# Copies inside a branch that is never taken, issued by GpSimd instead of ScalarE

## The chip, the cores and the metric

The kernel runs on one core of one Trainium2 chip. The metric is the device time of one execution in microseconds; of three runs the median is 1869.39 us (1868.79 to 1871.61). The profile is of one further execution, traced by the hardware profiler.

## The reference, cut to what matters

Two blocks follow each other on 256 tokens of width 1024. The first has two layers, each a token mixer (attention, then a pooling mixer) and a mixture of experts; the second block (recurrent mixers and dense feed-forward layers) is not touched. The change lies in the mixture of experts, which both layers have, each with weights of its own:

```python
scores = sigmoid(hf @ router_w)              # 256 tokens x 32 experts
e_idx  = top_k(where(best_group, scores + router_bias, -inf), 2)
gate   = scores[e_idx] / sum(scores[e_idx])
# every expert e, on the tokens that chose it:
y[e]   = (silu(x[e] @ w1[e]) * (x[e] @ w3[e])) @ w2[e]     # 1024 -> 512 -> 1024
out    = sum over the two chosen experts of gate * y[e]
```

Weights are drawn at random, so how many tokens choose one expert is not bounded by the shapes: the worst case is 256.

## The kernel before, in words

The 32 experts of a layer are worked off in 16 pairs (`for p in range(NPAIR)` in `experts`). Each expert gets 64 slots for tokens (`cap`), so that a pair fills the 128 partitions. For a pair TensorE runs

- `up` (L1190): the gathered tokens `hg` against w1 and w3, four chunks of weights of 2 MB, 16 matmuls for each chunk;
- `turned` (L1203): four transposes of the activated product `u`, which VectorE copies into the tile `uT` (L1205);
- `down` (L1217): `uT` against w2, two chunks of 2 MB, 16 matmuls for each; its two halves are written into the tiles `yh` (by ScalarE, L1228 in layer 0 and L1224 in layer 1) and `yl` (by VectorE, L1229 and L1226);
- `spread_out` (L1242 and L1237): adds the result to the tokens; it is done one pair later.

Every second pair the tokens of the next two pairs are gathered (L1155, with `oh` made by VectorE at L1141 and L1144). TensorE's order is that of the code; the other engines' instructions are ordered by a scheduler.

**The stream of weights.** All chunks of the kernel stand in one list. `prefetch` (L206) issues the next one from SyncE (SP) as soon as one of the rings `ringa`, `ringb`, `ringc` has a free slot (ten slots in layer 0, seven in most of layer 1). Each of these DMAs raises one of eight semaphores, DMAHW0 to DMAHW7, taken in turn, and waits for the DMA that used the same semaphore eight places earlier; so at most eight are in flight.

**The overflow branch.** Where an expert gets more than 64 tokens, the rest is computed in `overflow`, called once in each layer, in pair 9 after `up` and before `turned`. It loads the largest count into a register on every engine (L1287) and branches (L1288). The body uses the tiles `hg`, `oh`, `uT`, `yh` and `yl` as its own, so that the instructions behind the branch which write these tiles wait for the body's copies. Those copies (L1299, L1313, L1318, L1325) use DMA semaphores like any other DMA. On the way that leaves the body out, the semaphores that the body would have raised are raised by hand, so that both ways end at the same counts: each by one instruction that first waits until the semaphore stands at the count at which the body would have found it. With the counts of this input neither layer takes the branch: no instruction of its body shows in the trace.

Of the kernel before, what the change touches and what calls it, by code (L numbers as in the profile page):

```python
# [19 lines left out]
T = 256  # L20
# [144 lines left out]
class Net:  # L165
# [1112 lines left out]
    def overflow(self, l, htok, gate, slot, mint, cap, yacc, wp, pp):  # L1278


        nc, tc, A = self.nc, self.tc, self.A
        h = wp.tile([128, KT, T], F32, name="hg")
        idr = wp.tile([128, 2, 4, 64], F32R, name="oh").rearrange("p a b n -> p (a b n)")[:, 0:128]
        ug = wp.tile([128, 4, 128], F32, name="uT").rearrange("p a n -> p (a n)")
        u, gr = ug[:, 0:T], ug[:, T:2 * T]
        w, wd = (wp.tile([128, D], F32, name=n) for n in ("yh", "yl"))
        rv = nc.values_load(mint[0:1, 0:1], min_val=0, max_val=T)  # L1287
        with tc.If(rv > cap):  # L1288
            with ExitStack() as es:
                dp = es.enter_context(tc.tile_pool(name=f"ovd{l}", bufs=1, space=DRAM))  # L1290
                rows = dp.tile([NE, T], F32, name="rows")
                nc.scalar.copy(idr, self.ident)
                ov, rsb = w[:, 0:2 * NE].rearrange("p (a e) -> p a e", a=2), wd[0:NE, 0:T]
                nc.vector.scalar_tensor_tensor(ov, slot, float(cap), gate, op0=OP.is_gt, op1=OP.mult)
                pr = pp.tile([NE, T], F32, name="e1", bufs=2)
                for tt in range(2):
                    nc.tensor.transpose(pr[:, tt * 128:(tt + 1) * 128], ov[:, tt, :], self.ident)
                nc.vector.tensor_copy(rsb, pr)
                nc.scalar.dma_start(rows, rsb)  # L1299
                for k in range(KT):  # L1300
                    ph = pp.tile([128, T], F32, name="e1", bufs=2)
                    for tt in range(2):
                        for i in range(2):
                            nc.tensor.matmul(ph[:, tt * 128:(tt + 1) * 128], htok[i][:, tt, k * 128:(k + 1) * 128], idr,
                                             start=i == 0, stop=i == 1)
                    nc.vector.tensor_scalar(h[:, k, :], ph, self.mscale[l][:, 1, k:k + 1], self.shift(l, 1)[:, k:k + 1],
                                            op0=OP.mult, op1=OP.add)
                wk = w.rearrange("p (k n) -> p k n", k=KT)
                we = A["exp"][l].rearrange("q c p (a b n) -> q c p a b n", a=4, b=2)
                with tc.For_i(0, NPAIR, 1) as pv:  # L1310
                    for ab in range(2):
                        src = rows[:, :].rearrange("(q a) t -> q a t", a=2)[ds(pv, 1), ab, :]
                        nc.scalar.dma_start(gr, src.to_broadcast([128, T]))  # L1313
                        for ft in range(4):
                            ps = []
                            for i in range(2):
                                for c in range(2):
                                    nc.scalar.dma_start(  # L1318
                                        wk[:, 4 * c:4 * c + 4, :],
                                        we[ds(pv, 1), 2 * i + c, :, :, ab, ft * 128:(ft + 1) * 128]  # L1320
                                        .rearrange("q p a n -> (q p) a n"))
                                ps.append(pp.tile([128, T], F32, name="e0", bufs=2))
                                self.dense(ps[i], wk, 0, h)
                            for hf in range(2):
                                nc.scalar.dma_start(wd[:, 512 * hf:512 * hf + 512],  # L1325
                                                  we[ds(pv, 1), 4 + hf, :, ft, ab, :].rearrange("q p n -> (q p) n"))
                            nc.scalar.activation(u, ps[0], AF.Silu)
                            nc.vector.tensor_tensor(u, u, ps[1], op=OP.mult)
                            nc.vector.tensor_tensor(u, u, gr, op=OP.mult)
                            if l:  # L1330
                                nc.vector.tensor_tensor(wd, wd, self.gb, op=OP.mult)
                                for tt in range(2):
                                    for hf in range(2):
                                        nc.tensor.matmul(yacc[tt][hf], u[:, tt * 128:(tt + 1) * 128], wd[:, 512 * hf:512 * hf + 512],
                                                         start=False, stop=False, skip_group_check=True)
                            else:
                                for nt in range(KT):
                                    nc.tensor.matmul(yacc[:, nt, :], wd[:, nt * 128:(nt + 1) * 128], u,
                                                     start=False, stop=False, skip_group_check=True)
# [1078 lines left out]
```

## Time and profile before

| | |
|---|---|
| time, median of three runs | 1869.39 us |
| the profiled execution | 1871.96 us |
| its span, first to last instruction | 1870.2 us |
| TensorE's granted clock, mean | 0.967 of full speed |
| TensorE busy | 1738.4 us, 93% of the span |
| VectorE, ScalarE, GpSimd busy | 791.0, 532.7, 163.6 us |
| read from HBM | 579.65 MB, 311 GB/s over the span |

TensorE passes the branch at 476 us of the span in layer 0 and at 975 us in layer 1. A row of a timeline or a wait names the engine, the line of the kernel and the tile that is written; `SPq` is SyncE's own instruction queue. A value in brackets is the idle time of the engine just before, and what ended it.

### The profile page before, as it was taken

How to read it: one execution, taken by the hardware profiler on the slowest of the kernel's cores; microseconds unless marked ns; L12 is line 12 of the kernel's file. 1: busy time of each engine (PE TensorE's matmuls, PEld its weight loads, DVE VectorE, ACT ScalarE, POOL GpSimd, SP SyncE). 2: the span in 40 equal slices, each digit the busy share in tenths (PEclk: the TensorE clock that was granted, in tenths of full speed). 3: DMA queues.
4: the chain of work that ended last, by engine and by line, in shares of the span. 5: the costliest groups of instructions: out<-in, count | busy, mean ns of one | idle time of the engine just before them, and what ended most of it. 6: DMA issues, size and time to landing. Idle time of an engine off the chain costs nothing. (4 is left out here: it accounts for less than half of the span.)

```text
span 1870.2 us, 26586 instructions
## 1 busy us (share of the span) xinstructions
PE 1738.4 (93%) x11262; PEld 1165.4 (62%) x11262; DVE 791.0 (42%) x1552; ACT 532.7 (28%) x950; POOL 163.6 (9%) x249
## 2 busy tenths in 40 slices
PE   6998999999589989999995999999999999999998
PEld 4666544443234445444433434779999989989997
DVE  4687422211112125222522242665655566565554
ACT  2321211111001122111200101445644466564443
POOL 0000000000000000000440340223000002200000
PEclk9999999999789999999997999989999999999999
DMA  9998899999999996999996999615344533344531
GB/s 397 426 422 317 366 427 427 426 428 426 426 390 426 426 428 273 421 426 410 427 426 273 421 413 426 256 68 193 150 177 180 196 143 136 136 158 181 214 127 66
DMA packets 41665, 582.52 MB, mean 311 GB/s; under 512 B 4625, under 2 KB 4753, under 8 KB 5953
## 3 DMA queue, kind: packets, MB, share of 16 engines
q1 hardware_dynamic: 41328, 580.46, 75.1%
q8 instruction: 92, 1.51, 0.3%
q10 hardware_dynamic: 208, 0.26, 0.1%
q14 instruction: 37, 0.30, 0.0%
HBM read 579.65 MB, written 1.05 MB: 311 GB/s over the span
## 5 line engine op out<-in xcount | busy, mean ns | idle before, releaser
L243 DVE TENSOR_TENSOR wlo<-ringa,whi 128x1024 fp32r<-128x1024 f32 x192 | 228.5, 1231 | 174.6 <-ACT whi L242 174.6
L1190 PE MATMUL e<-ringb,hg 128*64 128x512 f32 x1056 | 233.9, 594 | 1.2 <-DMA ringb<-in_exp 1.2
L242 ACT CAST whi<-ringa 128x1024 fp32r<-128x1024 f32 x192 | 191.4, 1050 | 144.2 <-issue 54.9
L266 PE MATMUL ph<-hlo,whi 128*128 128x256 f32 x704 | 198.8, 282 | 1.2 <-DVE hlo L557 1.2
L265 PE MATMUL ph<-hhi,whi 128*128 128x256 f32 x704 | 198.6, 282 | 0.0
L267 PE MATMUL ph<-hhi,wlo 128*128 128x256 f32 x704 | 198.4, 282 | 0.0
L1197 DVE TENSOR_TENSOR u<-u,e 128x512 f32<-128x512 f32 x32 | 22.0, 688 | 384.1 <-PE e L1190 384.1
L1190 PEld LDWEIGHTS e<-ringb,hg 128*64 128x64 f32 x1056 | 79.6, 137 | 146.2 <-issue 141.8
L1190 PE MATMUL e<-ringa,hg 128*64 128x512 f32 x592 | 134.2, 599 | 17.7 <-DVE yl L1229 16.0
L266 PEld LDWEIGHTS ph<-hlo,whi 128*128 128x128 f32 x704 | 133.9, 190 | 2.4 <-DVE hlo L557 1.6
L265 PEld LDWEIGHTS ph<-hhi,whi 128*128 128x128 f32 x704 | 133.9, 190 | 0.8
L267 PEld LDWEIGHTS ph<-hhi,wlo 128*128 128x128 f32 x704 | 133.9, 190 | 0.0
L1467 POOL TENSOR_TENSOR ringa<-ringa 128x128 f32<-128x128 f32 (+1 forms) x86 | 45.8, 545 | 813.5 <-DVE ringa L1463 703.3
L1217 PE MATMUL e<-ringa,uT 128*64 128x512 f32 x384 | 91.4, 623 | 19.4 <-DVE uT L1205 15.8
L1190 PEld LDWEIGHTS e<-ringa,hg 128*64 128x64 f32 x592 | 45.1, 138 | 100.9 <-issue 81.7
L1217 PE MATMUL e<-ringb,uT 128*64 128x512 f32 x416 | 95.8, 606 | 8.8 <-DVE uT L1205 7.2
L1190 PE MATMUL e<-ringc,hg 128*64 128x512 f32 x400 | 88.4, 592 | 1.8 <-DMA ringc<-in_exp 1.8
L1228 ACT ACTIVATE yh<-e,gs 128x512 fp32r<-128x512 f32 x32 | 21.9, 687 | 226.0 <-PE e L1217 195.3
L1160 ACT ACTIVATE hg<-e,mod,msc 128x256 f32<-128x256 f32 x64 | 36.2, 565 | 164.9 <-DVE hg L1162 157.1
L1224 ACT CAST yh<-u 128x512 fp32r<-128x512 f32 x32 | 19.8, 618 | 217.6 <-DVE u L1223 217.6
L1155 PE MATMUL e<-oh,hth 128*128 128x256 f32 x256 | 68.9, 305 | 12.1 <-DVE oh L1141 7.5
L1229 DVE SCALAR_TENSOR_TENSOR yl<-e,gs,yh 128x512 fp32r<-128x512 f32 x32 | 23.9, 750 | 123.7 <-ACT yh L1228 123.7
(588 smaller groups left out, 3209.5 us busy)
## 6 DMA issues: line engine op xcount, KB each, us to landing
ringb<-in_exp SPq DMA_DIRECT2D x92, 2048.0 KB, 20.0
ringa<-in_exp SPq DMA_DIRECT2D x61, 2048.0 KB, 19.7
ringc<-in_exp SPq DMA_DIRECT2D x39, 2048.0 KB, 24.0
ringa<-in_f SPq DMA_DIRECT2D x32, 2048.0 KB, 7.5
ringb<-in_ada SPq DMA_DIRECT2D x15, 2048.0 KB, 16.2
ringa<-in_ada SPq DMA_DIRECT2D x9, 2048.0 KB, 21.9
ringa<-in_cin SPq DMA_DIRECT2D x8, 2048.0 KB, 7.4
ringa<-in_attn SPq DMA_DIRECT2D x3, 2048.0 KB, 28.2
```

What stands on the lines that cost most here:

```text
L242: nc.scalar.copy(hi[:, o], raw[:, o])
L243: (eng or nc.vector).tensor_tensor(lo[:, o], raw[:, o], hi[:, o], op=OP.subtract)
L265: mm(ps, wh, ah, start=start, stop=False, **kw)
L266: mm(ps, wh, al, start=False, stop=False, **kw)
L267: mm(ps, wl, ah, start=False, stop=stop, **kw)
L1155: nc.tensor.matmul(pd[:, i, :], htok[h][:, tt, k * 128:(k + 1) * 128], oh[:, tt, :], start=tt + h == 0, stop=tt + h == 2)
L1160: nc.scalar.activation(hg[q][:, k, :], pd[:, i, :], AF.Identity, scale=sc[:, k:k + 1], bias=sh[:, k:k + 1])
L1190: nc.tensor.matmul(ps[s, :], h[:, kt, o:o + 64], w[:, k, ab, :], start=kt == 0, stop=kt == KT - 1)
L1197: nc.vector.tensor_tensor(u, u, ph[1], op=OP.mult)
L1217: nc.tensor.matmul(py[s, :], uT[:, ft, s], w[:, ft, ab, :], start=ft == 0, stop=ft == 3)
L1229: nc.vector.scalar_tensor_tensor(lo, py, g, hi, op0=OP.mult, op1=OP.subtract)
L1467: nc.gpsimd.tensor_tensor(o, a, b, op=op)
```

## The change

The four kinds of copies in the branch's body are issued by GpSimd (POOL) instead of ScalarE. DMAs that GpSimd issues use another set of eight semaphores, DMASW0 to DMASW7.

```diff
                 nc.vector.tensor_copy(rsb, pr)
-                nc.scalar.dma_start(rows, rsb)
+                nc.gpsimd.dma_start(rows, rsb)
...
                     for ab in range(2):
                         src = rows[:, :].rearrange("(q a) t -> q a t", a=2)[ds(pv, 1), ab, :]
-                        nc.scalar.dma_start(gr, src.to_broadcast([128, T]))
+                        nc.gpsimd.dma_start(gr, src.to_broadcast([128, T]))
...
-                                    nc.scalar.dma_start(
+                                    nc.gpsimd.dma_start(
                                         wk[:, 4 * c:4 * c + 4, :],
...
-                                nc.scalar.dma_start(wd[:, 512 * hf:512 * hf + 512],
+                                nc.gpsimd.dma_start(wd[:, 512 * hf:512 * hf + 512],
```

SyncE's queue in layer 0, from the end of the branch on, before (the first row is the way around the body; `ringb_3084` is the next weight chunk):

```order
L1288 UNCONDITIONAL_BRANCH [waits DMAHW0_49,DMAHW1_49,DMAHW2_49,DMAHW3_49,DMAHW4_49,DMAHW5_49,DMAHW6_49,DMAHW7_49]
L206 DMA ringb_3084<-in_exp 128x4096 [waits DMAHW3_49,PE_49]
L206 DMA ringb_3097<-in_exp 128x4096 [waits DMAHW4_49,PE_49]
L206 DMA ringa_3110<-in_exp 128x4096 [waits DMAHW5_49,DMAHW0_49,PE_49]
L206 DMA ringa_3120<-in_exp 128x4096 [waits DMAHW6_49,DMAHW1_49,PE_49]
```

The same place after the change:

```order
L1288 UNCONDITIONAL_BRANCH
L206 DMA ringb_3084<-in_exp 128x4096 [waits DMAHW0_49,PE_49]
L206 DMA ringb_3097<-in_exp 128x4096 [waits DMAHW1_49,PE_49]
L206 DMA ringa_3110<-in_exp 128x4096 [waits DMAHW2_49,PE_49]
L206 DMA ringa_3120<-in_exp 128x4096 [waits DMAHW3_49,PE_49]
```

The eight waits at the end of the branch are gone; the DMAs keep their order.

VectorE's queue behind the branch in layer 0, before (`uT_3071` and `yl_3074` belong to pair 9):

```order
L1144 TENSOR_TENSOR oh_3169<-oh_3169,gate_1350 128x256 [waits DVE_49]
L1205 COPY uT_3071<-e1_3066 128x512 [waits DMAHW2_49,PE_49]
L1144 TENSOR_TENSOR oh_3169<-oh_3169,gate_1350 128x256 [waits DVE_49]
L1229 SCALAR_TENSOR_TENSOR yl_3074<-e0_3075,gs_2299,yh_3073 128x512 [waits DMAHW1_49,DMAHW2_49,DMAHW0_49,Activation_49]
L1229 SCALAR_TENSOR_TENSOR yl_3074<-e0_3088,gs_2299,yh_3073 128x512 [waits Activation_49]
```

And after:

```order
L1144 TENSOR_TENSOR oh_3169<-oh_3169,gate_1350 128x256 [waits DVE_49]
L1205 COPY uT_3071<-e1_3066 128x512 [waits DMASW2_49,PE_49]
L1144 TENSOR_TENSOR oh_3169<-oh_3169,gate_1350 128x256 [waits DVE_49]
L1229 SCALAR_TENSOR_TENSOR yl_3074<-e0_3075,gs_2299,yh_3073 128x512 [waits DMASW1_49,DMASW2_49,DMASW0_49,Activation_49]
L1229 SCALAR_TENSOR_TENSOR yl_3074<-e0_3088,gs_2299,yh_3073 128x512 [waits Activation_49]
```

The order is the same; the waits on the body's copies now ask for the other set of semaphores. ScalarE's copy into `yh` changes in the same way.

GpSimd's queue at the end of the branch in layer 1, before (what follows is its work for the second block):

```order
L1288 UNCONDITIONAL_BRANCH
L1467 TENSOR_TENSOR ringa_4749<-ringa_4749 128x4x32 [waits PE_49] x2
L1467 TENSOR_TENSOR ringa_4749<-ringa_4749 128x4x32 [waits Pool_49]
L1467 TENSOR_TENSOR ringa_4749<-ringa_4749 128x4x32 [waits PE_49] x2
L1467 TENSOR_TENSOR ringa_4749<-ringa_4749 128x128 [waits Pool_49]
```

And after:

```order
L1288 ISA [waits DMASW4_49,DMASW5_49,DMASW3_49,DMASW6_49,DMASW2_49,DMASW7_49,DMASW1_49,DMASW0_49]
L1288 UNCONDITIONAL_BRANCH
L1467 TENSOR_TENSOR ringa_4749<-ringa_4749 128x4x32 [waits PE_49] x2
L1467 TENSOR_TENSOR ringa_4749<-ringa_4749 128x4x32 [waits Pool_49]
L1467 TENSOR_TENSOR ringa_4749<-ringa_4749 128x4x32 [waits PE_49] x2
```

One instruction has come in, at the end of the way around the body (in layer 0 too): it raises the eight DMASW semaphores (`INC_SWDGE_SEM` in the trace). In layer 0 the counts that it waits for are zero, in layer 1 those that its own instance in layer 0 has left; no other DMA of the kernel uses this set. The body on GpSimd has grown by about a hundred rows in each layer, that on ScalarE has shrunk by as many.

## Rows read from the trace of the kernel before

**Rows 1.** The page's second part: busy tenths of the DMA engines in 40 slices

```profile
DMA  9998899999999996999996999615344533344531
```

**Rows 2.** All instructions of L1288: count, duration in ns (min/median/max), first and last start

```profile
L1288 SPq EVENT_SEMAPHORE  x16: 17/17/17, 486.6 to 1003.8; - x16
L1288 POOLq COMPARE_BRANCH  x2: 45/45/45, 208.4 to 956.7; - x2
...
L1288 PEldq COMPARE_BRANCH  x2: 6019/6028/6037, 476.0 to 975.2; - x2
```

**Rows 3.** SyncE's waits, 470 to 540 and 975 to 1035: total us, times, longest

```profile
SPq L1288 <- SPq L1288: 38.7, 8, 5.0
...
SPq L1288 <- SPq L1288: 25.2, 1, 25.2
```

**Rows 4.** SyncE's timeline in layer 0: start, us to the group's end, instruction

```profile
432.63 10.13 SPq L206 DMA_DIRECT2D ringb<-in_exp  x3
...
481.74 40.09 SPq L206 DMA_DIRECT2D ringb<-in_exp  x3
...
635.82 0.33 SPq L206 DMA_DIRECT2D ringc<-in_exp  x1
```

**Rows 5.** DMAs issued at 481.74 and at 635.82: last column us to landing

```profile
ringb<-in_exp SPq DMA_DIRECT2D x1, 2048.0 KB, 39.1
...
ringc<-in_exp SPq DMA_DIRECT2D x1, 2048.0 KB, 26.3
```

**Rows 6.** TensorE's timeline around the branch of layer 0

```profile
466.98 3.65 PE L1190 MATMUL e<-ringa,hg 128*64 128x512 f32 x16 [1.33 <-DMA ringa<-in_exp]
...
497.29 9.30 PE L1217 MATMUL e<-ringb,uT 128*64 128x512 f32 x32 [7.19 <-DVE uT L1205]
522.54 8.62 PE L1190 MATMUL e<-ringa,hg 128*64 128x512 f32 x32 [15.95 <-DVE yl L1229]
```

**Rows 7.** VectorE's timeline there

```profile
490.34 0.42 DVE L1144 TENSOR_TENSOR oh<-oh,gate 128x256 f32<-128x256 f32 x1
496.54 0.69 DVE L1205 COPY uT<-e 128x512 f32<-128x512 f32 x1 [5.78 <-SPq L1288]
```

**Rows 8.** ScalarE's timeline there

```profile
521.01 1.27 ACT L1228 ACTIVATE yh<-e,gs 128x512 fp32r<-128x512 f32 x2 [30.66 <-SPq L1288]
```

**Rows 9.** TensorE's timeline at the end of layer 0's experts

```profile
663.22 3.63 PE L1190 MATMUL e<-ringc,hg 128*64 128x512 f32 x16
...
670.19 7.09 PE L1217 MATMUL e<-ringc,uT 128*64 128x512 f32 x32
```

**Rows 10.** Stretches: start:end, length, busy us by engine, PEclk, DMA share, GB/s

```profile
524.00:660.00 136.00, 133.10 (x684) 60.38 (x682) 23.81 (x41) 14.38 (x23) 0.00 (x0) 0.99 1.01 427
...
714.00:729.00 15.00, 14.01 (x98) 10.42 (x100) 10.93 (x39) 2.45 (x5) 0.00 (x0) 1.00 0.01 1
...
1000.00:1012.00 12.00, 7.65 (x22) 2.29 (x24) 2.73 (x5) 0.19 (x1) 0.00 (x0) 0.57 0.11 48
1012.00:1033.00 21.00, 18.04 (x282) 8.85 (x280) 4.38 (x11) 1.65 (x3) 0.00 (x0) 0.92 0.76 290
1033.00:1180.00 147.00, 142.08 (x808) 64.55 (x806) 48.31 (x109) 15.17 (x25) 42.75 (x100) 1.00 1.00 422
```

**Rows 11.** VectorE's timeline around the branch of layer 1

```profile
988.80 0.42 DVE L1144 TENSOR_TENSOR oh<-oh,gate 128x256 f32<-128x256 f32 x1
1003.60 0.69 DVE L1205 COPY uT<-e 128x512 f32<-128x512 f32 x1 [14.38 <-SPq L1288]
```

**Rows 12.** TensorE's timeline there

```profile
1004.35 6.63 PE L1217 MATMUL e<-ringa,uT 128*64 128x512 f32 x16 [15.78 <-DVE uT L1205]
...
1040.43 3.65 PE L1217 MATMUL e<-ringa,uT 128*64 128x512 f32 x16 [0.39 <-issue]
```

**Rows 13.** The instruction at the program's start that raises DMASW semaphores

```profile
L2410 POOLq INC_SWDGE_SEM  x1: 27/27/27, 0.1 to 0.1; - x1
```

**Rows 14.** GpSimd's timeline behind the branch of layer 1

```profile
1048.32 3.46 POOL L1467 TENSOR_TENSOR ringa<-ringa 128x128 f32<-128x128 f32 x8 [91.58 <-PE e L1530]
```

## The prediction

> **What bounds the kernel now.** I read the busy tenths by slices first, then the instructions of the branch's line, SyncE's waits, the timelines of SyncE, TensorE, VectorE and ScalarE around the two places where the branch stands, and last a table by stretches. The slices show DMA engines that are full through nearly all of the experts [rows 1]; the stage of the change is a stream of weights with matmuls close behind. In layer 0 the stream is the bound: SyncE issues ten chunks from 432.63 to 481.74, one every 4.91 us, each one taking 39.1 us to land [rows 4, 5], that is eight in flight, while TensorE works 3.65 us on a chunk and then waits 1.33 us for the next one [rows 6].
>
> Into this stream falls the branch. Nobody takes it, yet SyncE runs its 16 EVENT_SEMAPHOREs, eight for each layer [rows 2], and waits 38.7 us in all at those of layer 0 and 25.2 us at those of layer 1 [rows 3]. The first starts at 486.6, and 486.6 is 481.74 plus one step of the stream; eight waits of up to 5.0 us follow, one step each. So each of the eight waits for one of the chunks in flight, and SyncE is held until the pipe is empty. Two kinds of work pay. First, the tiles of pair 9: VectorE's copy into `uT` and ScalarE's write of `yh` need the counts that SyncE raises so late [rows 7, 8, 11], and TensorE needs both. Second, the stream itself runs dry once: the DMA issued at 481.74 is followed only after it has landed.
>
> **The change part by part.** *Taken away: SyncE's eight waits.* The order shows the next chunk directly behind the jump, waiting only for the chunk eight places ahead and for its slot. *Taken away: the waits of `uT`, `yh`, `yl` on SyncE.* They ask for the other set, raised by GpSimd, which reaches its branch at 208.4 in layer 0 and at 956.7 in layer 1 [rows 2], long before 490.8 and 989.2, when VectorE is otherwise ready. *Moved: the body's DMAs and GpSimd's body.* None of it is executed. On ScalarE the body goes; nothing that ScalarE does there ended a wait.
>
> Layer 0. Without the stream as a limit TensorE would gain all that it now loses. `uT` would be copied at 490.76 (the end of L1144) instead of 496.54: 5.78 us [rows 7]. Then 15.95 us in front of L1190 [rows 6], which is the wait on `yl` behind ScalarE's `yh`. Then the two slow groups behind these gaps: 9.30 against 7.09 us for the same 32 matmuls at the layer's end, and 8.62 against twice 3.63 [rows 6, 9]: 2.21 + 1.36. In all 25.3 us. But the stream cannot follow: between 524 and 660 its share is 1.01 at 427 GB/s [rows 10], so it gains only its own bubble. Continued at 4.91 us from the chunk that lands at 481.74 + 39.1 = 520.84, the layer's last chunk, 28 places later (now issued at 635.82, landed at 662.1), lands at 520.84 + 28 x 4.91 = 658.3. The chunk two places ahead, the last of L1190, lands at 648.5; TensorE is through it 3.63 us later, at 652.1. From there to the end of the last L1217 it is now 677.28 - 666.85 = 10.43 us [rows 9], which gives 662.5; the last chunk itself allows 658.3 + 3.55 = 661.9, so it does not bind. Gain: 677.28 - 662.5 = **14.7 us**. It comes from the bubble (3.8 us) and from 11 us by which chunks now lie ready before TensorE needs them: the chunk landed at 662.1 is used from 673.7 on. The gain is handed on whole: from 714 to 729 the DMA engines stand at a share of 0.01 [rows 10], so all slots are full and the next chunk goes out when TensorE frees one.
>
> Layer 1. `uT` is ready to be copied at 989.22 and is copied at 1003.60: 14.38 us [rows 11]. The first chunk behind takes 6.63 us instead of 3.65 [rows 12], at a granted clock of 0.57 in that stretch [rows 10], close to the lower of the two levels: 2.98 us. Together **17.4 us**. Is there a stream to carry it? It now idles 0.89 x 12 + 0.24 x 21 = 15.7 us in the two stretches after 1000 and runs at a share of 1.00 with TensorE busy 142.08 of 147 us after that [rows 10]. These 15.7 us come back, and the missing 1.7 is less than a chunk's lead; I take 17.4 and keep 15.7 as the lower bound.
>
> Added: one instruction on GpSimd in each layer. The same kind took 27 ns at the start of the program [rows 13]. How long it takes for eight semaphores to be seen elsewhere no row shows. From below it is 27 ns; the longest that anything here took from issue to being marked done is 39.1 us, a 2 MB transfer behind seven others [rows 5]. I take the small value, since it is the row of this very instruction. The cover is 989.2 - 956.7 = 32.5 us in layer 1 (both ends move by layer 0's gain) and 282 us in layer 0. Of what stands behind that instruction GpSimd's next work waits 91.58 us for TensorE anyway [rows 14].
>
> One thing can make GpSimd later: its way around the body now spans some hundred rows. A jump around the body costs GpSimd 45 ns now, and TensorE 6.03 us [rows 2]. The Trainium skill (Runtime: NRT & Kernel Launch, Instruction fetch mechanics) says that a taken branch whose target is outside the fetched window must wait for a fetch; by it GpSimd's 45 ns could become TensorE's 6.03, which leaves 26 of the 32.5 us and the sum as it is.
>
> Sum: 14.7 + 17.4 = 32.1 us. The profiled execution took 1871.96 us, which becomes 1839.9. It lies 2.57 us over the median of the runs; from 1869.39 it gives **1837.3 us**, 1.7% faster.
>
> **Rivals.**
> *The stream hides layer 0's gain.* If the chunks were no earlier to use than to land, layer 0 would gain the bubble, 3.8 us, and layer 1 its 15.7: 1849.9. For it: the share of 1.01. Against it: the 11 us for which the last chunk lies ready.
> *The clock falls in the gaps.* Layer 0's last pairs will again wait for each chunk, for 4.91 - 3.65 = 1.3 us. For it: after the 15.78 us gap a chunk took 6.63 us. Against it: with gaps of 1.33 us chunks still took 3.65 [rows 6]. A fall costs 2.98 us and ends itself, since a chunk of 6.63 us leaves no gap. Two of them: 1843.3. The Trainium skill (TensorE: Matmul & The Clock Gate, HAM oscillation) tells of a kernel in which each wait for a slice of weights sets the clock down again; the rows here show waits that do not.
> *GpSimd's mark comes late.* At 39.1 us after its branch it would cost 39.1 - 32.5 = 6.6 us in layer 1: 1843.9.
> *It comes so late that the kernel is slower.* That needs 32.5 + 32.1 = 64.6 us from GpSimd's branch to the count being seen. Were the mark to take as long as GpSimd's longest wait there, 91.58 us, `uT` would be 59.1 us late: 1896. The order speaks against it: the mark stands ahead of that wait.
> *Nothing changes,* because the waits stay in another shape: 1869. SyncE's queue in the new order has none.
>
> **How the numbers follow.** The forecast gets 0.78, the stream 0.06, the clock 0.06, the late mark 0.04, the very late one 0.03, no change 0.03. Faster by over 0.2% (3.7 us, about what a measurement can tell here): 0.94; within: 0.03; slower: 0.03. Low end: the last chunk allows 677.28 - 661.9 = 15.4 in layer 0, so 1836.6; the runs before reach from 0.6 below to 2.2 above their median, and gathers that now run slowly beside the waits may run faster, for which I allow 6 us, about the three slow groups above (2.21 + 1.36 + 2.98 = 6.6): 1830. High end: the two rivals at 1843 to 1844 and nearly the first: 1848. That is 0.9 of the chance if the estimate of sizes is fair, and I count it as 0.8.
>
> **What would show it.** Right: no wait of SyncE at L1288; an issue every 4.9 us from 482 to 521; L1205 of pair 9 at about 491 and, 14.7 earlier in layer 1, at about 974.5; 32 matmuls of L1217 in about 7.1 us; a DMA share of 1.0 across both branches; TensorE waiting again for single chunks toward the end of layer 0. Wrong: a wait of L1205 or L1228 on POOL's L1288; rows of TensorE at half speed in layer 0's last pairs; layer 0's experts ending later than 663; layer 1 waiting for chunks behind the branch.

## The result, and the profile after

The changed kernel takes 1840.11 us (median of four runs, 1839.22 to 1841.73), the kernel before 1869.09 us beside it (four runs). The ratio is 0.9845, with a 95% interval of 0.9828 to 0.9862. Predicted were 1837.3 us, in a range of 1830 to 1848.

The profiled execution has a span of 1837.6 us against 1870.2. Where the difference arises, by four places that both traces have:

| place | before, us | after, us | ahead by |
|---|---|---|---|
| end of the last L1217 of layer 0 | 677.28 | 663.62 | 13.7 |
| uT of pair 9, layer 1 (L1205) | 1003.60 | 975.36 | 28.2 |
| first matmul behind layer 1's experts (L1785) | 1190.53 | 1159.44 | 31.1 |
| span | 1870.2 | 1837.6 | 32.6 |

The last 1.5 us come in the second block, which is the same in both. The medians lie 29.0 us apart: the profiled execution before took 2.9 us more than the median beside it (1871.96 against 1869.09), this one 0.9 less (1839.22 against 1840.11). The sum of the prediction was built on that one execution.

All instructions of the branch's line in the changed kernel (as [rows 2]):

```profile
L1288 POOLq EVENT_SEMAPHORE  x8: 17/43/43, 213.5 to 948.4; - x8
L1288 POOLq COMPARE_BRANCH  x2: 45/48/50, 208.2 to 943.0; - x2
L1288 POOLq INC_SWDGE_SEM  x2: 150/162/173, 213.8 to 948.5; - x2
...
L1288 PEldq COMPARE_BRANCH  x2: 5952/6030/6108, 475.8 to 961.5; - x2
...
L1288 SPq COMPARE_BRANCH  x2: 45/48/50, 482.0 to 964.3; - x2
```

SyncE's 16 EVENT_SEMAPHOREs are gone; GpSimd has one INC_SWDGE_SEM for each layer, done at 948.7 in layer 1. The copies into `uT` (answering to [rows 7, 11]) have no wait in front of them any more:

```profile
490.20 0.41 DVE L1144 TENSOR_TENSOR oh<-oh,gate 128x256 f32<-128x256 f32 x1
490.54 0.68 DVE L1205 COPY uT<-e 128x512 f32<-128x512 f32 x1
...
975.03 0.42 DVE L1144 TENSOR_TENSOR oh<-oh,gate 128x256 f32<-128x256 f32 x1
975.36 0.68 DVE L1205 COPY uT<-e 128x512 f32<-128x512 f32 x1
```

TensorE, behind the branch of layer 0, in layer 0's last pairs, and behind the branch of layer 1 ([rows 6, 9, 12]):

```profile
491.28 7.09 PE L1217 MATMUL e<-ringb,uT 128*64 128x512 f32 x32 [1.29 <-DVE uT L1205]
...
581.09 3.65 PE L1190 MATMUL e<-ringb,hg 128*64 128x512 f32 x16 [2.31 <-DMA ringb<-in_exp]
585.94 3.65 PE L1190 MATMUL e<-ringa,hg 128*64 128x512 f32 x16 [1.19 <-DMA ringa<-in_exp]
...
649.51 3.65 PE L1190 MATMUL e<-ringc,hg 128*64 128x512 f32 x16 [1.16 <-DMA ringc<-in_exp]
...
656.53 7.09 PE L1217 MATMUL e<-ringc,uT 128*64 128x512 f32 x32
...
976.10 3.65 PE L1217 MATMUL e<-ringa,uT 128*64 128x512 f32 x16 [1.29 <-DVE uT L1205]
```

Both L1217 run at full speed at once. From 575 on TensorE waits for single chunks, which it did not do there before: layer 0 is bound by the stream up to its end. Chunks still take 3.65 us behind these waits. The stretches say the same of the DMA engines (the last three numbers: PEclk, DMA share, GB/s):

```profile
476.00:521.00 45.00, 37.78 (x194) 19.72 (x194) 10.45 (x21) 4.92 (x8) 0.00 (x0) 0.92 1.01 426
...
524.00:660.00 136.00, 122.25 (x626) 53.84 (x624) 20.49 (x36) 13.01 (x21) 0.00 (x0) 1.00 1.01 427
```

### The profile page after: what moved, and what is told of

Its sections match the earlier page's. It is cut to its first block, busy times and chain, and to the rows that moved or that the text cites. A ratio compares the mean times of both kernels' runs of the same rounds, so it can differ in the third digit from the quotient of the medians.

```text
span 1837.6 us, 26585 instructions
## 1 busy us (share of the span) xinstructions
PE 1730.5 (94%) x11262; PEld 1161.7 (63%) x11262; DVE 790.7 (43%) x1552; ACT 533.1 (29%) x950; POOL 164.1 (9%) x249
## 5 line engine op out<-in xcount | busy, mean ns | idle before, releaser
L1190 PE MATMUL e<-ringb,hg 128*64 128x512 f32 x1056 | 234.2, 595 | 6.2 <-DMA ringb<-in_exp 6.2
L1190 PEld LDWEIGHTS e<-ringb,hg 128*64 128x64 f32 x1056 | 80.0, 138 | 151.7 <-issue 142.4
L1190 PE MATMUL e<-ringa,hg 128*64 128x512 f32 x592 | 133.1, 594 | 6.1 <-DMA ringa<-in_exp 6.0
L1190 PEld LDWEIGHTS e<-ringa,hg 128*64 128x64 f32 x592 | 44.0, 137 | 89.7 <-issue 83.2
L1217 PE MATMUL e<-ringb,uT 128*64 128x512 f32 x416 | 93.6, 594 | 2.9 <-issue 1.6
L1217 PE MATMUL e<-ringa,uT 128*64 128x512 f32 x384 | 88.4, 606 | 4.9 <-issue 3.6
L1190 PE MATMUL e<-ringc,hg 128*64 128x512 f32 x400 | 88.4, 593 | 3.0 <-DMA ringc<-in_exp 3.0
L1194 ACT ACTIVATE u<-e 128x512 f32<-128x512 f32 x32 | 19.1, 597 | 196.8 <-PE e L1190 196.8
```

The source lines that it names most:

```text
L1190: nc.tensor.matmul(ps[s, :], h[:, kt, o:o + 64], w[:, k, ab, :], start=kt == 0, stop=kt == KT - 1)
L1217: nc.tensor.matmul(py[s, :], uT[:, ft, s], w[:, ft, ab, :], start=ft == 0, stop=ft == 3)
```

## The experiments

The first theory was that of the prediction: each layer loses by itself what SyncE's eight waits hold up. A ratio is to the kernel before, in the runs beside which a group ran; its medians there are 1869.97 us (one layer at a time, SyncE's waits alone, all on `nc.sync`), 1871.18 (turned semaphores, no branch) and 1871.0 (late mark). The range behind a ratio is its 95% interval.

**One layer at a time.** The edit of the first kernel; the second has `l == 1`.

```diff
+        dq = nc.gpsimd if l == 0 else nc.scalar
...
-                nc.gpsimd.dma_start(rows, rsb)
+                dq.dma_start(rows, rsb)
...
```

> Layer 0's copies on GpSimd, layer 1's on ScalarE as before. Theory (each layer's wait on the stream of weights is its own loss): layer 0's experts end near 663.6 as with the whole change, layer 1 keeps its wait of about 14 us in front of uT, and the time is 1869.1 - 13.7 = 1855.4 (1853 to 1858). Rival (the stream hides layer 0's gain): 1865. Rival (the gain is one thing that needs both layers, as a shorter body on ScalarE for the whole program): 1840 or 1869.

> Layer 1's copies on GpSimd, layer 0's on ScalarE as before. Theory: layer 0's experts end near 677.3 as before, layer 1 gives 14.4 us of wait and 3.0 us of the slow chunk, 1869.1 - 17.4 = 1851.7 (1849 to 1854). Rival (layer 1 only wins what layer 0 left over of the stream's lead): 1855 or more.

Layer 0 alone: 1840.28 us (ratio 0.9832, 0.9806 to 0.9858), the whole gain and not 13.7 us of it. Layer 1 alone: 1854.14 us (0.9908, 0.9873 to 0.9942), 15.8 us instead of 17.4. The two gains sum to 45.5 us where both together give 29: the theory of two independent losses falls. The traces say in which layer: layer 1's stretch from this row on (its place before the change)

```profile
742.66 0.79 PE L1171 MATMUL e<-ident,oh 128*128 128x128 f32 x4 [2.23 <-DVE oh L1144]
```

to the first matmul behind its experts is 447.9 us before and 430.5 after the change, 430.4 with layer 1 alone changed, and 432.9 with layer 0 alone: 14.9 of layer 1's 17.4 us come back with none of layer 1's copies moved. With layer 0 alone changed, SyncE still waits at its marks in layer 1 (L1289 there), as long as before:

```profile
SPq L1289 <- SPq L1289: 25.7, 6, 5.4
```

but in six waits of up to 5.4 us, where [rows 3] has a single one of 25.2. That is what I had read over. The marks (the instructions that raise the semaphores by hand) are made in a fixed order, DMAHW0 first. Before, in layer 1, the first of them fell on the newest chunk in flight (issued at 977.58, landed at 1003.2), and the other seven stood behind it, also the one that `uT` asks for, whose chunk, issued at 957.74, had landed 21.0 us later, at 978.7:

```profile
ringa<-in_exp SPq DMA_DIRECT2D x1, 2048.0 KB, 21.0
```

Which chunk falls on which semaphore depends on how many DMAs of the set stand before it in the program, those of a body that is never executed included. Without layer 0's body, the chunks of layer 1 lie three semaphores further back and `uT` asks for another one. Its row in VectorE's order, before and with layer 0 alone changed:

```
L1205 COPY uT_5887<-e1_5882 128x512 [waits DMAHW3_49,PE_49]
L1205 COPY uT_5887<-e1_5882 128x512 [waits DMAHW0_49,PE_49]
```

The new theory: what the marks cost depends on how the stream's turn through the eight semaphores stands to their fixed order. A second thing is in the same trace: ScalarE's write of `yh` still waits 14.36 us for SyncE's marks, and TensorE still waits for little of it.

```profile
993.51 0.62 ACT L1224 CAST yh<-u 128x512 fp32r<-128x512 f32 x1 [14.36 <-SPq L1289]
```

```profile
PE e L1190 <- DVE yl L1226: 2.3, 1, 2.3
```

Between `down` and the next `up` it has matmuls for the second block to do there (L1531 and L1536, from 987.22 on). So in layer 1 the loss lies in what `uT` waits for; the same marks cost little when only `yh` stands behind them.

**Turning the semaphores without taking a copy off the set.** First, layer 0 alone on GpSimd and three small copies on ScalarE added to its body, which turn layer 1's chunks back to where they were before:

```diff
+                if l == 0:
+                    ex = dp.tile([8, 64], F32, name="ex")
+                    for j in range(3):
+                        nc.scalar.dma_start(ex[j:j + 1, :], self.ident[j:j + 1, 0:64])
```

> As the version with layer 0's copies alone on GpSimd, with three small copies on ScalarE added to layer 0's body (never executed): SyncE marks three semaphores in layer 0, those of the three oldest chunks in flight, and in layer 1 the chunks fall on the semaphores on which they fell before the change (newest chunk on the one that is marked first). New theory (layer 1's loss comes from the order of the marks: the first mark waits for the newest chunk, and all others stand behind it): layer 1 waits again about 14 us in front of uT, 1840.3 + 16 = 1856 (1853 to 1859). Rival (layer 1's wait went with layer 0's for another reason, as the later start of its stream): 1840.

It takes 1856.93 us (0.9925, 0.9902 to 0.9949): three copies that are never executed cost 16.6 us, and layer 1's stretch is 447.6 us again. SyncE has its single wait again, and `uT` stands behind it:

```profile
SPq L1289 <- SPq L1289: 25.2, 1, 25.2
```

```profile
990.59 0.69 DVE L1205 COPY uT<-e 128x512 f32<-128x512 f32 x1 [13.65 <-SPq L1289]
```

Then the kernel before, every copy on ScalarE, with one or five small DMAs that are executed at the program's start (the five stand under `l == 1`; SyncE issues both versions' from 13 us on) and turn both layers:

```diff
+            if l == 0:
+                ex = es.enter_context(tc.tile_pool(name="exd", bufs=1, space=DRAM)).tile([8, 64], F32, name="ex")
+                for j in range(1):
+                    nc.sync.dma_start(ex[j:j + 1, :], self.ident[j:j + 1, 0:64])
```

> The kernel before with one small DMA added at the program's start on SyncE (256 bytes), which moves every later chunk by one semaphore. New theory: in layer 0 the semaphore that is marked first now belongs to the newest chunk in flight instead of the oldest, so uT is released near 521 instead of 496.5 and TensorE's next pair starts 8 us later; layer 1 as before: 1870 + 8 = 1878 (1875 to 1881). First theory (SyncE waits until the pipe is empty, whatever the order): 1870.

> The same with five such DMAs. New theory: layer 0 as bad as with one (uT near 521), and in layer 1 the semaphore that is marked first belongs to the oldest chunk in flight, so uT is released at once and layer 1's 16 us come back with every copy still on ScalarE: 1870 + 8 - 16 = 1862 (1859 to 1865). First theory: 1870.

With one: 1875.30 us (1.0019, 1.0008 to 1.0031), slower than before. In layer 0 all eight marks now wait for the newest chunk (SyncE's waits, then `uT`):

```profile
SPq L1292 <- SPq L1292: 38.7, 1, 38.7
```

```profile
521.47 0.69 DVE L1209 COPY uT<-e 128x512 f32<-128x512 f32 x1 [30.28 <-SPq L1292]
```

The next pair's L1190 starts at 531.08 instead of 522.54. Of these 8.5 us, 7.0 are left behind layer 0's experts (L389: 690.12 against 683.13) and 4.6 in layer 1 (L1432: 908.88 against 904.29), so the price is smaller than the 8 expected. 1.6 us come back at once, since those 32 matmuls take 7.03 us where they took 8.62 [rows 6]. Another 1.7 come back behind a gap of 2.2 us that both have at the start of layer 1; the matmuls and their stretch, before, then with one DMA:

```profile
743.38 5.35 PE L1217 MATMUL e<-ringa,uT 128*64 128x512 f32 x16
743.00:749.00 6.00, 6.00 (x23) 1.94 (x24) 2.18 (x5) 0.00 (x0) 0.00 (x0) 0.72 1.01 434
...
749.92 3.65 PE L1221 MATMUL e<-ringa,uT 128*64 128x512 f32 x16
749.50:755.50 6.00, 6.00 (x29) 2.17 (x31) 3.09 (x6) 0.62 (x1) 0.00 (x0) 1.00 1.01 431
```

The granted clock of the stretch is 0.72 before, so that a part of it ran at the lower of the two levels (1.2 and 2.4 GHz), and 1.00 with one DMA; why is not shown. With five: 1857.54 us (0.9937, 0.9918 to 0.9956), 1.5 us below the range expected, since layer 0's loss was the same smaller one. Layer 1's wait is gone although all copies are still on ScalarE and SyncE still waits 25 us in all:

```profile
SPq L1292 <- SPq L1292: 25.3, 6, 4.9
```

```profile
992.48 0.68 DVE L1209 COPY uT<-e 128x512 f32<-128x512 f32 x1
```

One DMA and five differ by 17.8 us. In layer 0 both hold `uT` alike (30.28 and 30.15 us); in layer 1 they differ in which chunk falls on the semaphore that is marked first, and the stretch of layer 1 is 445.4 us with one and 430.5 with five. By the first theory both would have taken 1870.

**SyncE's waits without the tiles' waits.** The changed kernel with eight small copies on ScalarE at the body's start, which touch none of the tiles:

```diff
+                for j in range(8):
+                    nc.scalar.dma_start(ex[j:j + 1, :], self.ident[j:j + 1, 0:64])
```

> All copies of the body on GpSimd, and eight more small ones on ScalarE at the body's start that write a scratch in DRAM from a constant tile: SyncE has its eight waits at the branch again, but uT, yh and yl do not wait for them. Theory (both waits cost, the tiles' more): SyncE is held until 521 in layer 0 and about 990 in layer 1; the stream has its bubbles back, about 3 us in layer 0 and 4 in layer 1, TensorE does not stop at uT: 1840.1 + 7 = 1847 (1844 to 1850). Rival (SyncE's drain is the whole cost): 1869. Rival (the tiles' waits are the whole cost): 1840.

1844.36 us (0.9854, 0.9826 to 0.9882), by the medians some 4 us over the changed kernel, though the two intervals overlap. SyncE waits as long as before, `uT` does not:

```profile
SPq L1288 <- SPq L1288: 38.6, 8, 4.9
```

```profile
491.48 0.68 DVE L1205 COPY uT<-e 128x512 f32<-128x512 f32 x1
```

The stream's bubble is there: the last L1217 of layer 0 ends at 667.29 against 663.62 in the changed kernel, 3.7 us later, of which 0.6 stood before the branch, and the first matmul behind layer 1's experts starts 3.9 us later (1163.37 against 1159.44). The other 25 us of the change's gain do not need SyncE's waits gone, only the tiles' waits on them.

**The other engine, the same semaphores.** All four copies on `nc.sync`:

> The four kinds of copies issued by SyncE itself: the body leaves ScalarE as with the change, but the semaphores are those of the weights. Theory (the set of semaphores is what counts): SyncE keeps its eight waits in each layer and the tiles theirs, 1869 (1866 to 1872). Rival (the gain comes from ScalarE's shorter program): 1840.

1871.11 us (1.0011, 0.9997 to 1.0025): no change. SyncE's waits are those of [rows 3], 38.7 us in eight and 25.2 in one. ScalarE's shorter program gives nothing; what counts is the set of semaphores, with the place in the turn through it.

**No branch at all.**

```diff
-                self.overflow(l, htok, gate, slot, mint, cap, yacc, wp, pp)
+                if False: self.overflow(l, htok, gate, slot, mint, cap, yacc, wp, pp)
```

> Neither layer has the branch (for counts up to 64, as here, the result is that of the kernel before): also no 6.0 us in which TensorE executes its branch. Theory (after the change the stream of weights is the bound of both layers): 1840.1, at most 1 us less. Rival (what the branch still costs TensorE comes on top): gaps of 5.2 and 2.3 us and slow gathers behind them, about 12 us, 1828.

1839.63 us (0.9839, 0.9810 to 0.9869), the changed kernel's time. TensorE's 6.0 us in the branch and its 5.2 us gap in front of the gather are gone, and it waits for chunks instead. TensorE's waits for DMAs from 412 to 660, first of the changed kernel, then without the branch:

```profile
PE e L1190 <- DMA ringb<-in_exp: 6.2, 5, 2.3
PE e L1190 <- DMA ringa<-in_exp: 5.8, 6, 1.3
PE e L1155 <- DVE oh L1141: 5.2, 1, 5.2
PE e L1190 <- DMA ringc<-in_exp: 3.0, 3, 1.2
```

```profile
PE e L1190 <- DMA ringb<-in_exp: 10.5, 8, 2.5
PE e L1190 <- DMA ringa<-in_exp: 5.9, 6, 1.3
PE e L1190 <- DMA ringc<-in_exp: 4.0, 4, 1.1
```

15.0 us of waiting for chunks become 20.4, about the 5.2 us that the gap gave back. So, as far as these intervals tell, the change has already taken all that the branch cost in this kernel, and no version with a branch can be expected to beat it by the branch alone.

**A late mark.** Additions on GpSimd ahead of its branch in layer 1, 60 and 160:

```diff
+        if l:
+            pad = wp.tile([128, 64], F32, name="pad")
+            nc.gpsimd.memset(pad, 0.0)
+            for _ in range(60):
+                nc.gpsimd.tensor_tensor(pad, pad, pad, op=OP.add)
```

> The changed kernel with 60 small additions (128 x 64) on GpSimd ahead of its branch in layer 1, some 0.35 us each by the 0.5 us of its 128 x 128 products: its mark comes about 21 us later than at 948.5. Theory (the mark has a cover of 975.4 - 948.7 = 26.7 us until uT is otherwise ready): still hidden, 1840 (1838 to 1843). Rival (uT waits for the mark's whole delay): 1861.

> The same with 160 additions, about 56 us: the mark comes 29 us after uT is otherwise ready. Theory: TensorE waits these 29 us in front of the first L1217 behind the branch, and 2 or 3 us more for its slow first chunk; SyncE's stream goes on until all slots are full: 1840 + 29 to 32 = 1869 to 1872. Rival (the mark does not hold uT): 1840.

1837.74 us (0.9827, 0.9789 to 0.9865) and 1838.66 us (0.9832, 0.9780 to 0.9885). Neither tells anything of a late mark: the scheduler put the additions into GpSimd's idle time from 662 us on, and the mark came no later, at 947.8 with 60 and at 942.2 with 160, where it had been at 948.5:

```profile
L1291 POOL TENSOR_TENSOR pad<-pad x160: 292/293/828, 662.1 to 723.0; 128x64 f32<-128x64 f32 x160
...
L1293 POOLq INC_SWDGE_SEM  x2: 150/164/177, 211.8 to 942.2; - x2
```

How long the mark could be delayed before `uT` waits for it was not shown.

## Why the prediction was right, and which of its reasons was not

*What bounds the kernel.* Right for layer 0: the marks waited for the chunks one after the other, `uT` for the third and `yh` for the eighth. For layer 1 the step "each of the eight waits for one of the chunks in flight" was wrong. There were six chunks in flight, and the first mark alone waited for the newest; that SyncE was held until the pipe was empty is right there too (25.2 us). `uT`'s own chunk had landed at 978.7, 10.5 us before `uT` could be copied otherwise. [rows 3] had said so, with 8 waits in layer 0 and 1 in layer 1; I read only the sums. The 14.4 us were therefore not the price of using the weights' set, but of one place in the turn through it, which layer 0's part of the change moves by itself. The forecast did not depend on this, since the change takes all marks away and the wait was read from its row; with layer 0 alone changed it did, and there the same reasoning missed by 15 us (1855.4 expected, 1840.28 measured).

*Layer 0, 14.7 us.* Measured 13.7. The rule (the smaller of what TensorE could gain, 25.3, and what the stream allows) held: TensorE waits for single chunks again from 575 on. The missing 1.0 us goes with one irregular step of the stream: SyncE issues at 575.05 and then at 581.11, 6.1 us instead of 4.9, and TensorE waits 2.31 us at 581.09 where its other waits for chunks in layer 0's last pairs are 0.68 to 1.34. What made the step long is not shown.

*Layer 1, 17.4 us.* Measured 31.1 - 13.7 = 17.4. The second chunk of L1217, first after the slow one, starts 31.2 us ahead, the first 28.2: the 2.98 us of the slow chunk came back as priced. Taken alone against a layer 0 as before, it was 15.8 by the medians, with an interval of some 6 us to either side; the trace of that run has 17.4 in layer 1's stretch (447.9 to 430.4).

*The mark.* Its 27 ns were 150 to 173 ns in this place, with 26.7 us of cover (975.36 - 948.7) instead of the 32.5 expected: GpSimd needed 5.4 us from its branch (943.0) to the last EVENT_SEMAPHORE behind it (948.4). The prediction had allowed for this with TensorE's row, 6.03 us, which is close. The sum is not touched. The Trainium skill (Runtime: NRT & Kernel Launch, Instruction fetch mechanics), which the prediction named here, puts such a delay down to a fetch of the target's instructions; no run here shows that a fetch took the 5.4 us.

*The rivals.* The stream hid 11.6 of the 25.3 us of layer 0 (10.6 by the forecast), not its whole gain. The clock did not fall in the waits for chunks: behind waits of 1.16 to 2.31 us, with 3.65 us of matmuls between them, chunks took 3.65 us at a granted clock of 1.00 (524 to 660). That speaks against this rival. The kernel of which the Trainium skill tells (TensorE: Matmul & The Clock Gate, HAM oscillation) loses its clock at each such wait; this trace does not. The size of a gap alone does not decide: behind the gap of 2.23 us at the start of layer 1, where TensorE had done only two groups of transposes, 16 matmuls took 5.35 us in the changed kernel too, at a granted clock of 0.72 in their stretch:

```profile
729.64 5.35 PE L1217 MATMUL e<-ringa,uT 128*64 128x512 f32 x16
729.50:735.50 6.00, 6.00 (x22) 1.87 (x22) 2.42 (x5) 0.00 (x0) 0.00 (x0) 0.72 1.02 437
```

The late mark did not come; no run here forced it. Of the sum of 32.1 us the trace shows 31.1 up to the end of layer 1's experts.

## What to carry to other kernels

Instructions that raise semaphores by hand on the way around a branch are waits like any other, and in a chain of them in a fixed order each stands behind all that come earlier; so ask of each which DMA it follows, and which tile waits for it. If a rarely taken branch shares its DMA semaphores with a deep stream of loads, give it a set of its own; else its cost can change with any DMA that is added before it, executed or not. And read the count of a wait beside its sum: eight waits of 4.9 us and one of 25.2 are two mechanisms.

## What the runs showed of the hardware that was not expected

The way around the same body, from the branch to the last EVENT_SEMAPHORE behind it in layer 1, took GpSimd 5.4 us in the changed kernel (943.0 to 948.4), but 0.7 us in the kernel with 160 additions ahead of it (941.4 to 942.1). ScalarE's took 5.6 us before (466.2 to 471.8) and 0.1 us with its body gone (466.1 to 466.2). So the branch itself, 45 to 50 ns in its row, on these two engines tells little of what a jump costs; the start of the next instruction does. What made GpSimd's way short in the one kernel and long in the other is not shown.
